# Six RMS norms of a two-block transformer kernel: squares added on VectorE before TensorE sums their partitions

## The chip, the cores and the metric

The kernel runs on one core of a Trainium2 chip. The core has a matrix engine (TensorE, PE in the profile), a vector engine (VectorE, DVE), a scalar engine (ScalarE, ACT), GpSimd (POOL) and SyncE (SP), which here issues most of the DMAs. Each engine takes its instructions in a fixed order and stops where one has to wait for another engine. Matrix products go to PSUM, everything else lies in SBUF. The metric is the device time of one execution in microseconds (us).

## The reference

A first block (convolution and attention, then a product-key mixture of experts called peer) and a second block of two layers, on 256 tokens of 1024 features. Ahead of nearly every sublayer stands the same norm, whose result is scaled and shifted:

```python
def rms_norm(x, g):
    xf = x.astype(jnp.float32)
    y = xf * lax.rsqrt(jnp.mean(xf * xf, axis=-1, keepdims=True) + EPS)
    return (y * g.astype(jnp.float32)).astype(x.dtype)

def modulate_2(h, shift, scale):
    return h * (1 + scale[:, None, :]) + shift[:, None, :]

    for layer in range(DEPTH_2):        # cut from second_block
        if layer == N_A_LAYERS:
            k_sh, v_sh, F_sh = shared_kv(x, c_act, kv_ada_w, kv_ada_b, kv_norm_g, kv_w, fgate_w, fgate_b)
        h = modulate_2(rms_norm(x, norm_g[layer, 0]), sh1, sc1)
        x = x + 0.5 * g1[:, None, :] * swiglu(h, ffn_w_in[layer, 0], ffn_w_out[layer, 0])
        h = modulate_2(rms_norm(x, norm_g[layer, 1]), sh2, sc2)
        ...                             # mix = diff_attention(h, ...) or forgetting_attention(h, ...)
        x = x + g2[:, None, :] * mix
        h = modulate_2(rms_norm(x, norm_g[layer, 2]), sh3, sc3)
        x = x + 0.5 * g3[:, None, :] * swiglu(h, ffn_w_in[layer, 1], ffn_w_out[layer, 1])
```

## The kernel before

The program runs through the stages mix, peer, f00, diff, f01, kv, f10, forget and f11. The fNN are the feed-forward sublayers, diff and forget the two attentions, kv makes the keys, values and forget gate that forget uses. The stream X lies in SBUF as eight tiles of 128 features by 256 tokens (KT = 8, P = 128, T = 256), so the sum over the features of one token runs over the eight tiles and over the partitions of each.

Products are made with split operands: a weight chunk of 128x1024 comes by DMA into `raw`, ScalarE rounds it to `whi`, VectorE makes the rest `wlo = raw - whi`, and TensorE adds hi x hi, lo x hi and hi x lo. A product of one chunk with all of X is 24 matmuls of 128x256 (258 with two columns for the shift) and is called a unit here; its result lies in one PSUM buffer. Two buffers of the pool `ps_mm` and one or two of others hold such results, so a further unit can't start until an earlier one's buffer has been read.

A norm is begun by `norm_begin` (line 480). It makes `xg`, X times the gain, split in hi (ScalarE) and lo (VectorE), with a high scheduling priority (NPRIO = 400). ScalarE then squares X, one tile 128x256 at a time, into `sq`, and TensorE multiplies each with a matrix of ones: the eight `ss` matmuls, in plain fp32, add up the squares over all features and put the sum of each token on every partition. ScalarE takes the root, VectorE the reciprocal, which gives `rstd`, called `r` in the code.

The first units of the stage don't wait for `rstd`. They multiply the weights with `xg`, which is not normalised, and `fixed` (line 530) puts it right afterwards on VectorE: `fixb` copies the column of the shift out of PSUM, `fix` multiplies the product with `rstd`. When both have read it, the PSUM buffer is free. These units are called `wq` in peer, `qkv` in diff, `gux` in the feed-forwards, `kvu` in kv and `bq` in forget. Meanwhile `norm_steps` (line 540) makes the normalised h, tile by tile, over a scratch tile `nt`, for all later units.

`norm_begin` is called by peer (line 1605), the feed-forwards (line 590), diff (747), kv (907) and forget (1025). With `fin`, in f00, it also makes the final norm of the first block, with sixteen `ss`. f10 has no norm of its own; kv's serves it. The order of instructions on each engine is set ahead of time by a scheduler, which takes what it holds to be ready by its own estimates, and by priorities (`high_priority`; FPRI = 100 for `fixed`). On the chip that order is fixed. All operations go through one helper, so nearly every row of the profile has line L263.

Of the kernel before, what the change touches and what calls it, by code (L numbers as in the profile page):

```python
# [9 lines left out]
F32 = mybir.dt.float32  # L10
# [4 lines left out]
AF = mybir.ActivationFunctionType  # L15
# [5 lines left out]
P = 128  # L21
T = 256
D = 1024
KT = 8
# [125 lines left out]
class Ring:  # L150


    def __init__(self, pool, n):
        self.order = [pool] * n
        self.n = n
# [126 lines left out]
class Kern:  # L282
# [3 lines left out]
    def __init__(self, nc, tc, ins, out, phases, ctx):  # L286
        self.nc, self.tc, self.ins, self.out, self.ctx = nc, tc, ins, out, ctx
        self.phases = phases
        e = ctx.enter_context
        self.p_const = e(tc.tile_pool(name="const", bufs=1))  # L290
        self.r_raw = Ring(e(tc.tile_pool(name="raw", bufs=self.NRAW)), self.NRAW)
        self.r_w = Ring(e(tc.tile_pool(name="wsplit", bufs=self.LOOK + 1)), self.LOOK + 1)
        self.p_h = e(tc.tile_pool(name="hsplit", bufs=1))
        self.p_s = e(tc.tile_pool(name="small", bufs=2))
        self.ps_mm = e(tc.tile_pool(name="ps_mm", bufs=2, space=PSUM))
        self.ps_bg = e(tc.tile_pool(name="ps_bg", bufs=2, space=PSUM))
        self.bg = []
        self.gprio = {}
        self.late = []
        self.ada_done = {}  # L300
        self.ada_raw = {}
        self.cb2 = self.ada_last = None
        self.prio = 0
        self.lead = {"s": [], "v": [], "t": []}
        self.pace, self.paces = {}, {}
        self.nc = PacedNC(self, nc)
        self.xg = self.p_n = self.masks = None
        self.h_ready = self.fin_pending = False


# [169 lines left out]
    def norm_begin(self, pool, G, sh, xg, fin=None, psq=None):  # L480


        nc = self.nc
        hi, lo = xg
        x = self.X
        sh2 = pool.tile([P, KT, 2], F32, tag="sh2", name="sh2", bufs=1)
        nc.vector.memset(sh2, 0.0)
        nc.vector.tensor_copy(sh2[:, :, 0], sh)
        nc.scalar.activation(hi[:, :, T:], sh2, AF.Copy)
        nc.vector.tensor_sub(lo[:, :, T:], sh2, hi[:, :, T:])  # L490
        Gx = G
        if fin is not None:
            Gx = self.p_s.tile([P, 8], F32, tag="gcol", name="gcolx")
            nc.vector.tensor_mul(Gx, G, fin)
        n = 1 if fin is None else 2
        ps = self.ps_bg.tile([P, n, T], F32, tag="bg", name="ss")
        nc.scalar.activation(pool.tile([P, 1], F32, tag="sqw", name="sqw", bufs=1), self.eps, AF.Sqrt)
        with self.tc.high_priority(offset=NPRIO):
            for kt in range(KT):
                nc.scalar.activation(hi[:, kt, :T], x[:, kt], AF.Copy, scale=Gx[:, kt:kt + 1])  # L500
                nc.vector.scalar_tensor_tensor(lo[:, kt, :T], x[:, kt], Gx[:, kt:kt + 1], hi[:, kt, :T],
                                               op0=ALU.mult, op1=ALU.subtract)
        fsq = None
        if fin is not None:
            fsq = pool.tile([P, KT], F32, tag="fsq", name="fsq", bufs=1)
            nc.vector.tensor_mul(fsq, fin, fin)
        for kt in range(KT):
            sq = (psq or pool).tile([P, T], F32, tag="sq", name="sq", bufs=8 if psq else 4)
            nc.scalar.activation(sq, x[:, kt], AF.Square)
            for j in range(n):  # L510
                w = fsq[:, kt:kt + 1].to_broadcast([P, P]) if j else self.ones
                nc.tensor.matmul(ps[:, j], w, sq, start=kt == 0 and j == 0, stop=kt == KT - 1, skip_group_check=n > 1)
        r = pool.tile([P, T], F32, tag="rstd", name="rstd", bufs=1)
        r0 = pool.tile([P, T], F32, tag="r0", name="r0", bufs=1)
        with self.tc.high_priority(offset=NPRIO):
            if fin is None:
                nc.scalar.activation(r0, ps[:, 0], AF.Sqrt, scale=1.0 / D, bias=self.eps)
                nc.vector.reciprocal(r, r0)
                return Gx, r

            ms = pool.tile([P, T], F32, tag="ms", name="ms", bufs=1)
            nc.vector.tensor_scalar(ms, ps[:, 0], 1.0 / D, EPS, op0=ALU.mult, op1=ALU.add)
            m2 = pool.tile([P, T], F32, tag="ms2", name="ms2", bufs=1)
            nc.vector.tensor_scalar(m2, ms, EPS, None, op0=ALU.mult)
            nc.vector.scalar_tensor_tensor(m2, ps[:, 1], 1.0 / D, m2, op0=ALU.mult, op1=ALU.add)
            nc.scalar.activation(r0, m2, AF.Sqrt)
            nc.vector.reciprocal(r, r0)
        return Gx, r, ms
# [11 lines left out]
    def norm_steps(self, pool, x, G, sh, hi, lo, r):  # L540
        nc = self.nc
        for kt in range(KT):
            t = pool.tile([P, T], F32, tag="nt", name="nt", bufs=4)
            nc.vector.scalar_tensor_tensor(t, x[:, kt], G[:, kt:kt + 1], r, op0=ALU.mult, op1=ALU.mult)
            nc.scalar.activation(hi[:, kt], t, AF.Identity, bias=sh[:, kt:kt + 1])
            nc.vector.scalar_tensor_tensor(lo[:, kt], t, sh[:, kt:kt + 1], hi[:, kt], op0=ALU.add, op1=ALU.subtract)
            yield
# [1504 lines left out]
```

## Time and profile before

| | us |
|---|---|
| three runs | 2185.59, 2186.04, 2186.75; median 2186.04 |
| the profiled execution: time, and its span | 2187.28, 2185.5 |
| TensorE busy (matmuls) | 2152.6, 98% of the span |
| VectorE busy | 1763.1, 81% |
| ScalarE busy | 1202.3, 55% |
| granted TensorE clock, mean | 0.997 |

All durations come from the profiled execution. Its time is 1.78 us above its span. The chain of waits is the work that ended last, followed back in time step by step. A row of a timeline or of a group gives an instruction as `out<-in` with the shape and type, and behind it, in brackets, the idle time before it and what ended that. An fp32 matmul with plain operands leaves two records, one with split operands leaves one.

### The profile page before, as it was taken

The numbers are of one execution on the slowest core, as the hardware profiler recorded it, in microseconds if no ns is written. First come the engines' busy times: TensorE is split into PE (matmuls) and PEld (weight loads), VectorE is DVE, ScalarE is ACT, GpSimd is POOL, SyncE is SP. The second block draws the span as 40 slices with busy tenths as digits, with TensorE's granted clock in tenths as the row PEclk, the third lists the DMA queues.
The fourth block names the chain that finished last, engine by engine and source line by source line (L and its number), as shares of the span: only waits on it lengthen the run. The fifth ranks groups of instructions, "written<-read, shape, count | busy, mean of one in ns | idle before, by whom it ended". The sixth has DMA issues, their size and how long they took to land.

```text
span 2185.5 us, 39500 instructions
## 1 busy us (share of the span) xinstructions
PE 2152.6 (98%) x16034; PEld 2021.8 (93%) x16034; DVE 1763.1 (81%) x3214; ACT 1202.3 (55%) x1946; POOL 11.4 (1%) x26
## 2 busy tenths in 40 slices
PE   7999999999999999999999999999999999999998
PEld 4887899999999999999999999999999999999997
DVE  7779689987888777657779987879887899798665
ACT  5677665444434444444446556766556555576554
POOL 0000000000000000000000000000000000000000
PEclk9999999999999999999999999999999999999999
DMA  8246354545445988857776985436885688724551
GB/s 322 78 183 231 116 176 155 193 174 185 173 155 197 311 302 304 246 208 270 287 277 241 358 315 207 146 137 229 296 305 181 229 325 330 269 97 174 193 183 49
DMA packets 100631, 481.08 MB, mean 220 GB/s; under 512 B 40832, under 2 KB 41368, under 8 KB 44960
## 3 DMA queue, kind: packets, MB, share of 16 engines
q1 hardware_dynamic: 95744, 462.70, 58.7%
q10 hardware_dynamic: 3456, 10.90, 1.3%
q0 software_dynamic: 1248, 4.95, 0.6%
q8 instruction: 126, 2.06, 0.4%
q14 instruction: 57, 0.47, 0.1%
HBM read 469.05 MB, written 11.04 MB: 220 GB/s over the span
## 4 chain that ended last, share of the span: by engine, by line
PE 89%; DVE 7%; ACT 2%; issue 1%; DMA 1%; DVEq 0%; ACTq 0%
PE acc L263 28%; PE gu L263 20%; PE u L263 15%; PE win L263 4%; PE gps L263 3%; PE qkv L263 2%; PE gux L263 2%; DVE wlo L263 2%; PE pacc L263 2%; PE kvu L263 2%; PE ss L263 2%; PE sc L263 1%; PE po L263 1%; ACT whi L263 1%; DVE A L263 1%; PE outs L263 1%
## 5 line engine op out<-in xcount | busy, mean ns | idle before, releaser
L263 DVE TENSOR_TENSOR wlo<-raw,whi 128x1024 fp32r<-128x1024 f32 x650 | 794.1, 1224 | 233.6 <-ACT whi L263 228.7
L263 ACT ACTIVATE whi<-raw 128x1024 fp32r<-128x1024 f32 x650 | 686.5, 1057 | 483.9 <-PE acc L263 139.1
L263 PE MATMUL gu<-h,whi 128*128 128x512 f32 x1264 | 443.4, 393 | 0.0
L263 PE MATMUL u<-h,whi 128*128 128x256 f32 x2048 | 379.6, 284 | 1.6 <-ACT whi L263 1.6
L263 PE MATMUL gu<-h,wlo 128*128 128x256 f32 x1264 | 354.0, 280 | 0.0
L263 PEld LDWEIGHTS u<-h,whi 128*128 128x128 f32 x2048 | 322.9, 192 | 1.8 <-ACT whi L263 1.8
L263 PE MATMUL acc<-wh,whi 128*128 128x256 f32 x1024 | 289.8, 283 | 0.4 <-ACT wh L263 0.4
L263 PE MATMUL acc<-wh,wlo 128*128 128x256 f32 x1024 | 289.7, 283 | 0.0
L263 PE MATMUL acc<-wl,whi 128*128 128x256 f32 x1024 | 289.5, 283 | 0.0
L263 PEld LDWEIGHTS gu<-h,whi 128*128 128x128 f32 x1264 | 236.7, 187 | 50.2
L263 DVE SCALAR_TENSOR_TENSOR junk<-raw,crow 128x1024 f32<-128x1024 f32 x198 | 241.8, 1221 | 19.9 <-DMA raw<-wts 11.1
L263 PE MATMUL u<-h,wlo 128*128 128x256 f32 x1024 | 252.1, 284 | 0.2 <-DVE wlo L263 0.2
L263 PEld LDWEIGHTS gu<-h,wlo 128*128 128x128 f32 x1264 | 238.7, 189 | 0.0
L263 PE MATMUL acc<-ah,whi 128*128 128x256 f32 x704 | 197.6, 281 | 0.0
L263 PEld LDWEIGHTS acc<-wh,whi 128*128 128x128 f32 x1024 | 196.6, 192 | 0.6 <-ACT wh L263 0.6
L263 PEld LDWEIGHTS u<-h,wlo 128*128 128x128 f32 x1024 | 195.8, 191 | 1.2 <-DVE wlo L263 0.9
L263 PE MATMUL acc<-ah,wlo 128*128 128x256 f32 x704 | 196.9, 280 | 0.0
L263 PEld LDWEIGHTS acc<-wh,wlo 128*128 128x128 f32 x1024 | 196.6, 192 | 0.0
L263 PEld LDWEIGHTS acc<-wl,whi 128*128 128x128 f32 x1024 | 196.5, 192 | 0.0
L263 PE MATMUL acc<-al,whi 128*128 128x256 f32 x704 | 195.9, 279 | 0.4
L263 PEld LDWEIGHTS acc<-ah,whi 128*128 128x128 f32 x704 | 132.2, 188 | 3.4
L263 PEld LDWEIGHTS acc<-al,whi 128*128 128x128 f32 x704 | 132.1, 188 | 1.0 <-DVE al L263 1.0
(386 smaller groups left out, 3590.9 us busy)
## 6 DMA issues: line engine op xcount, KB each, us to landing
raw<-wts SPq DMA_DIRECT2D x427, 1024.0 KB, 5.0
G<-sp ACTq DMA_DIRECT2D x16, 512.0 KB, 3.0
gl<-G SPq DMA_DIRECT2D x16, 512.0 KB, 6.9
Fb<-fscr POOLq DMA_DIRECT2D x1, 2048.0 KB, 8.7
scr<-brow POOLq DMA_DIRECT2D x1, 1536.0 KB, 20.4
KR<-wts SPq DMA_DIRECT2D x1, 1024.0 KB, 10.9
KS<-wts SPq DMA_DIRECT2D x1, 1024.0 KB, 12.9
X<-xT SPq DMA_DIRECT2D x1, 1024.0 KB, 14.8
```

The source lines that it names most:

```text
L263: i = f(*a, **kw)
```

## The change

In the six norms without `fin` (peer, diff, f01, kv, forget, f11), ScalarE squares four tiles of X with one instruction into `sqn`, one tile of 128 x 8 x 256. VectorE adds them in place: tiles 2 and 3 to 0 and 1, 6 and 7 to 4 and 5, then 4 and 5 to 0 and 1, each with one instruction of 128x512. TensorE then sums the partitions of tiles 0 and 1 alone, with two `ss`. In f00 the eight squares and sixteen `ss` stay, with slices of `sqn` as their target. `norm_steps` uses the first four slices of `sqn` as its scratch once that tile exists.

```diff
--- before.py
+++ after.py
@@ -304,7 +304,7 @@
         self.lead = {"s": [], "v": [], "t": []}
         self.pace, self.paces = {}, {}
         self.nc = PacedNC(self, nc)
-        self.xg = self.p_n = self.masks = None
+        self.xg = self.p_n = self.masks = self.sqn = None
         self.h_ready = self.fin_pending = False
 
 
@@ -504,12 +504,24 @@
         if fin is not None:
             fsq = pool.tile([P, KT], F32, tag="fsq", name="fsq", bufs=1)
             nc.vector.tensor_mul(fsq, fin, fin)
-        for kt in range(KT):
-            sq = (psq or pool).tile([P, T], F32, tag="sq", name="sq", bufs=8 if psq else 4)
-            nc.scalar.activation(sq, x[:, kt], AF.Square)
-            for j in range(n):
-                w = fsq[:, kt:kt + 1].to_broadcast([P, P]) if j else self.ones
-                nc.tensor.matmul(ps[:, j], w, sq, start=kt == 0 and j == 0, stop=kt == KT - 1, skip_group_check=n > 1)
+
+        sqn = self.sqn = pool.tile([P, KT, T], F32, tag="sqn", name="sqn", bufs=1)
+        if fin is None:
+
+            for i in (0, 4):
+                nc.scalar.activation(sqn[:, i:i + 4], x[:, i:i + 4], AF.Square)
+                nc.vector.tensor_add(sqn[:, i:i + 2], sqn[:, i:i + 2], sqn[:, i + 2:i + 4])
+            nc.vector.tensor_add(sqn[:, 0:2], sqn[:, 0:2], sqn[:, 4:6])
+            for i in range(2):
+                nc.tensor.matmul(ps[:, 0], self.ones, sqn[:, i], start=i == 0, stop=i == 1)
+        else:
+            for kt in range(KT):
+                sq = sqn[:, kt]
+                nc.scalar.activation(sq, x[:, kt], AF.Square)
+                for j in range(n):
+                    w = fsq[:, kt:kt + 1].to_broadcast([P, P]) if j else self.ones
+                    nc.tensor.matmul(ps[:, j], w, sq, start=kt == 0 and j == 0, stop=kt == KT - 1,
+                                     skip_group_check=n > 1)
         r = pool.tile([P, T], F32, tag="rstd", name="rstd", bufs=1)
         r0 = pool.tile([P, T], F32, tag="r0", name="r0", bufs=1)
         with self.tc.high_priority(offset=NPRIO):
@@ -540,7 +552,7 @@
     def norm_steps(self, pool, x, G, sh, hi, lo, r):
         nc = self.nc
         for kt in range(KT):
-            t = pool.tile([P, T], F32, tag="nt", name="nt", bufs=4)
+            t = pool.tile([P, T], F32, tag="nt", name="nt", bufs=4) if self.sqn is None else self.sqn[:, kt % 4]
             nc.vector.scalar_tensor_tensor(t, x[:, kt], G[:, kt:kt + 1], r, op0=ALU.mult, op1=ALU.mult)
             nc.scalar.activation(hi[:, kt], t, AF.Identity, bias=sh[:, kt:kt + 1])
             nc.vector.scalar_tensor_tensor(lo[:, kt], t, sh[:, kt:kt + 1], hi[:, kt], op0=ALU.add, op1=ALU.subtract)
```

With other dependencies the scheduler also arrives at another order. First TensorE at the start of diff, before. `ss` are the sums of squares, `qkv_N` the units (`xg0` and `xg1` are the hi and lo part of X times gain, `whi` and `wlo` the weights); left out are the matmuls between.

```order
L263 MATMUL ss_15361<-sq_15380,ones_78 128x256
L263 MATMUL qkv_15427<-xg0_13151,whi_15230 128x258
...
L263 MATMUL ss_15361<-sq_15383,ones_78 128x256
L263 MATMUL qkv_15427<-xg0_13151,whi_15230 128x258
...
L263 MATMUL ss_15361<-sq_15386,ones_78 128x256
...
L263 MATMUL ss_15361<-sq_15401,ones_78 128x256
L263 MATMUL qkv_15427<-xg1_13152,whi_15230 128x258 x8
L263 MATMUL qkv_15464<-xg0_13151,whi_15253 128x258
...
L263 MATMUL qkv_15464<-xg1_13152,whi_15253 128x258 x8
L263 MATMUL qkv_15499<-xg0_13151,whi_15284 128x258
...
L263 MATMUL qkv_15499<-xg1_13152,whi_15284 128x258 x8
L263 MATMUL qkv_15536<-xg0_13151,whi_15288 128x258
```

The same place after:

```order
L263 MATMUL qkv_15387<-xg0_13142,whi_15206 128x258
...
L263 MATMUL qkv_15459<-xg1_13143,whi_15260 128x258 x8
L263 MATMUL qkv_15618<-xg0_13142,whi_15418 128x258
L263 MATMUL ss_15337<-sqn_15356,ones_78 128x256 x2
L263 MATMUL qkv_15618<-xg0_13142,wlo_15419 128x258
...
L263 MATMUL qkv_15618<-xg1_13143,whi_15418 128x258 x8
L263 MATMUL qkv_15496<-xg0_13142,whi_15264 128x258
```

The eight `ss` stood inside the first unit. The two stand behind three whole units and the first matmul of a fourth, `qkv_15618`. That is the unit which used to be further back: it has a PSUM buffer of another pool, and its 24 matmuls are pulled ahead of `qkv_15496`, the unit that needs the buffer of the first one.

VectorE at the same place, from the last splits of weights ahead of the reciprocal to the first two `fix`, before:

```order
L263 TENSOR_TENSOR wlo_15289<-raw_15058,whi_15288 128x1024
L263 TENSOR_TENSOR wlo_15424<-raw_15087,whi_15423 128x1024
L263 COPY fixb_15452<-qkv_15427 128x1
L263 RECIPROCAL rstd_15404<-r0_15405 128x256
L263 TENSOR_TENSOR wlo_15459<-raw_15087,whi_15458 128x1024
L263 TENSOR_TENSOR fix_15453<-qkv_15427,rstd_15404 128x256
L263 COPY fixb_15489<-qkv_15464 128x1
L263 TENSOR_TENSOR fix_15490<-qkv_15464,rstd_15404 128x256
```

And after, from the first `fixb` on:

```order
L263 COPY fixb_15412<-qkv_15387 128x1
L263 COPY fixb_15449<-qkv_15424 128x1
L263 TENSOR_TENSOR sqn_15356<-sqn_15356 128x512 x2
L263 TENSOR_TENSOR wlo_15384<-raw_15063,whi_15383 128x1024
L263 TENSOR_TENSOR sqn_15356<-sqn_15356 128x512
L263 COPY fixb_15484<-qkv_15459 128x1
L263 TENSOR_TENSOR wlo_15419<-raw_15063,whi_15418 128x1024
L263 TENSOR_TENSOR wlo_15456<-raw_15124,whi_15455 128x1024
L263 TENSOR_TENSOR wlo_15491<-raw_15124,whi_15490 128x1024
L263 RECIPROCAL rstd_15364<-r0_15365 128x256
L263 TENSOR_TENSOR wlo_15555<-raw_15178,whi_15554 128x1024
L263 TENSOR_TENSOR fix_15413<-qkv_15387,rstd_15364 128x256
```

One `wlo` stood between `rstd` and the first `fix`, and two ahead of `rstd`. Now the three additions stand among the `wlo`, three `wlo` come between the last addition and `rstd`, and `wlo_15555` stands ahead of `fix_15413`; its operand `whi_15554` is made by ScalarE in the buffer of `whi_15418`, which the unit `qkv_15618` reads. The second `fixb` stands ahead of the additions and reads the result of the second unit. forget and kv have the same pattern in this order.

VectorE at the start of f01, before:

```order
L263 TENSOR_TENSOR wlo_16966<-raw_16502,whi_16965 128x1024
L263 TENSOR_TENSOR wlo_17099<-raw_16610,whi_17098 128x1024
L263 RECIPROCAL rstd_17085<-r0_17086 128x256
L263 COPY fixb_17127<-gux_17102 128x1
L263 TENSOR_TENSOR wlo_17133<-raw_16610,whi_17132 128x1024
L263 TENSOR_TENSOR fix_17128<-gux_17102,rstd_17085 128x256
```

and after:

```order
L263 TENSOR_TENSOR wlo_16918<-raw_16454,whi_16917 128x1024
L263 COPY fixb_17063<-gux_17038 128x1
L263 TENSOR_TENSOR sqn_17013<-sqn_17013 128x512 x2
L263 COPY fixb_17105<-gux_17074 128x1
L263 TENSOR_TENSOR wlo_17035<-raw_16562,whi_17034 128x1024
L263 TENSOR_TENSOR sqn_17013<-sqn_17013 128x512
L263 TENSOR_TENSOR wlo_17069<-raw_16562,whi_17068 128x1024
L263 TENSOR_TENSOR wlo_17117<-raw_16708,whi_17116 128x1024
L263 RECIPROCAL rstd_17021<-r0_17022 128x256
L263 COPY fixb_17151<-gux_17120 128x1
L263 TENSOR_TENSOR fix_17064<-gux_17038,rstd_17021 128x256
```

Here `fixb_17105`, the copy from the second unit, and one `wlo` stand between the second and the third addition, and on TensorE the two `ss` follow right behind the second unit. f11 has the same order.

## Rows read from the trace of the kernel before

**Rows 1.** The page: busy time of the engines; shares of the chain by engine.
```profile
PE 2152.6 (98%) x16034; PEld 2021.8 (93%) x16034; DVE 1763.1 (81%) x3214; ACT 1202.3 (55%) x1946; POOL 11.4 (1%) x26
...
PE 89%; DVE 7%; ACT 2%; issue 1%; DMA 1%; DVEq 0%; ACTq 0%
```

**Rows 2.** Stretches: us; busy (instructions) of PE, PEld, DVE, ACT, POOL; clock, DMA share, GB/s.
```profile
20.00:38.90 18.90, 12.34 (x44) 4.85 (x42) 16.47 (x36) 8.70 (x14) 0.00 (x0) 1.00 0.79 281
38.90:45.80 6.90, 6.04 (x24) 5.45 (x25) 6.90 (x18) 2.56 (x5) 0.33 (x1) 0.51 0.92 381
345.00:365.00 20.00, 17.99 (x146) 17.36 (x146) 20.00 (x105) 8.73 (x15) 0.00 (x0) 1.00 0.36 125
352.00:358.00 6.00, 4.14 (x33) 3.94 (x34) 6.00 (x33) 2.85 (x5) 0.00 (x0) 1.00 0.29 90
1340.00:1400.00 60.00, 59.66 (x450) 56.72 (x450) 53.89 (x129) 44.98 (x106) 0.00 (x0) 1.00 0.40 141
1400.00:1480.00 80.00, 78.66 (x614) 74.91 (x615) 59.10 (x141) 56.34 (x141) 0.00 (x0) 1.00 0.37 133
1660.00:1700.00 40.00, 39.36 (x311) 37.62 (x311) 30.90 (x65) 28.66 (x50) 1.09 (x2) 1.00 0.43 153
1950.00:1985.00 35.00, 35.00 (x284) 32.22 (x284) 30.07 (x82) 21.92 (x56) 0.00 (x0) 1.00 0.34 122
```

**Rows 3.** The chain: start us, us, what; from peer, diff, f01, kv and forget.
```profile
307.05 1.01 DVE A L263 x4
...
1353.21 0.43 PE ss L263 x2
...
1356.26 2.59 PE ss L263 x12
1358.85 7.09 PE qkv L263 x59
1365.94 0.45 PE sc L263 x4
...
1477.60 1.29 PE ss L263 x6
...
1679.18 2.83 PE fgp L263 x24
...
1915.06 5.76 PE bq L263 x48
1920.82 1.31 PE sc L263 x8
```

**Rows 4.** Tiles: count, then ns min/median/max, first and last start in us.
```profile
L263 PE MATMUL ss<-sq,ones x144: 377/379/483, 19.6 to 2175.8; 128*128 128x256 f32 x144
...
L263 ACT ACTIVATE sq<-X x62: 401/404/422, 18.5 to 2173.1; 128x256 f32<-128x256 f32 x62
...
L263 DVE TENSOR_TENSOR A<-A,gl x32: 684/686/689, 712.5 to 920.4; 128x512 f32<-128x512 f32 x32
...
L263 DVE RECIPROCAL rstd<-r x9: 1744/1753/1755, 28.2 to 2176.7; 128x256 f32<-128x256 f32 x9
L263 DVE TENSOR_TENSOR fix<-qkv,rstd x9: 412/417/419, 1363.1 to 1389.1; 128x256 f32<-128x256 f32 x9
```

**Rows 5.** The page's costliest groups: busy us, mean ns, idle before and releaser.
```profile
L263 DVE TENSOR_TENSOR wlo<-raw,whi 128x1024 fp32r<-128x1024 f32 x650 | 794.1, 1224 | 233.6 <-ACT whi L263 228.7
L263 ACT ACTIVATE whi<-raw 128x1024 fp32r<-128x1024 f32 x650 | 686.5, 1057 | 483.9 <-PE acc L263 139.1
```

**Rows 6.** Timeline of VectorE where diff starts: start us, us, instruction [idle before].
```profile
1357.44 2.35 DVE L263 TENSOR_TENSOR wlo<-raw,whi 128x1024 fp32r<-128x1024 f32 x2
...
1360.35 1.75 DVE L263 RECIPROCAL rstd<-r 128x256 f32<-128x256 f32 x1 [0.34 <-ACT r L263]
```

**Rows 7.** Timeline of VectorE where peer starts.
```profile
302.56 1.75 DVE L263 RECIPROCAL A<-A 128x256 f32<-128x256 f32 x1 [1.80 <-ACT A L263]
...
304.75 0.41 DVE L263 TENSOR_TENSOR A<-wq,A 128x256 f32<-128x256 f32 x1
```

## The prediction

> **What bounds the kernel now.** First the page's busy times and the chain of waits: TensorE is busy for 2152.6 of 2185.5 us and carries 89% of the chain that ended last [rows 1]. A 98% average could hide stages with other limits, so next comes the table of stretches. Around five of the six norms TensorE is nearly full: 59.66 of 60 us where diff starts, 39.36 of 40 where kv starts, 35.00 of 35 at the end of forget [rows 2]. The exception is the routing in peer: between 345 and 365 us VectorE is busy for all 20 us and TensorE for 17.99 [rows 2], and the chain goes over VectorE there [rows 3]. So in five stages an instruction taken off TensorE gives its time back, provided that no new wait takes it, and in peer only what VectorE's line allows. The chain also shows that TensorE does not wait for the norm today: from the last `ss` at 1358.85 us it runs 59 `qkv` matmuls without a break [rows 3]. The products run on unnormalised X; 1/rms is multiplied in afterwards by `fix`, which frees a PSUM buffer. The room for that is what the change works with.
>
> **What is removed.** Six norms lose 6 of 8 `ss` matmuls, 36 in all. The trace has two records for each fp32 matmul (the 72 of the program with `sq` and `ones` are x144 [rows 4]), and 12 records take 2.59 us on the chain [rows 3]: 0.216 a record, 0.432 us a matmul. Per norm 6 x 0.432 = 2.59 us, in all 36 x 0.432 = 15.55 us of TensorE. ScalarE's 8 squares of 0.404 us become two of 128x1024; the row of that size is `whi` with 1.057 us [rows 4, 5], so 3.23 becomes 2.11 us a norm. ScalarE idles by turns around the norms, and that saving I count as nothing.
>
> **What is added.** Three VectorE additions 128x512 a norm. A row of that form and type exists, `A<-A,gl` with 0.686 us [rows 4]; queued ones start about 0.6 us apart by the overlap of the rows of [rows 6], where two `wlo` of 1.22 take 2.35. Some 2 us a norm, 12.3 us in all by the full duration. VectorE is off the chain in the five stages, so they cost what they delay.
>
> **What moves, and this decides.** The scheduler puts the pair of `ss` where it thinks the sums ready: behind 73 unit matmuls in diff, kv and forget, behind 48 in f01 and f11, behind 34 in peer; before it was inside the first unit. On VectorE the sums stand between splits of weights (`wlo`) and `COPY fixb`, which waits for the end of a unit on TensorE; RECIPROCAL then stands behind three more `wlo` (two in f01). The first `fix` comes later than the third PSUM buffer is full, and TensorE must stop, for the first time. One unit is 24 matmuls; 48 took 5.76 us in forget [rows 3], so 2.88 a unit.
>
> *diff.* TensorE starts its units at 1353.2 us, where the first `ss` stands now [rows 3]. With about 0.3 us for the late half of `xg` (a wide square stands between), unit 1 ends at 1359.3 and unit 2 at 1362.1. VectorE ends `xg` at 1357.4 [rows 6], does a `wlo` and waits for unit 1: COPY 1359.4, two additions 1360.7, `wlo` (1.15 queued) 1361.85, third addition 1362.5. `ss` waits 0.35 us and ends at 1363.4. Then COPY and the `wlo` of the unit pulled forward: 1363.8, again 0.35 us of wait. Two `wlo` more, 1366.1; RECIPROCAL 1.75 us [rows 4, 6], 1367.85. That unit ends at 1366.55 (1363.8 + 23 x 0.12); only then may its buffer take the next split: `whi` 1.06 to 1367.65, `wlo` to 1369.0, `fix` 0.42 [rows 4] to 1369.4. TensorE waits 1369.4 - 1366.55 = 2.85 us for its next PSUM buffer. New idle 3.55, saved 2.59: +0.95 us.
>
> *forget* has the same order of instructions and, by the same steps 0.35 + 0.35 + 2.9 = 3.6: +1.0.
>
> *f01.* Two units from 1477.6 [rows 3] end at 1483.4. The pair of `ss` comes next and needs COPY 0.15, `wlo` 1.2, addition 0.7 and the hand-overs: 2.15 us idle to 1485.5; `ss` to 1486.4, unit 2 to 1489.3. RECIPROCAL stands behind two `wlo`, 1487.8 to 1489.55, COPY and `fix` to 1490.1: 0.8 us idle. In all 2.95: +0.4. *f11* alike: 3.05, +0.45.
>
> *kv.* The same order on VectorE, but TensorE has the forget gate's 24 matmuls (2.83 us [rows 3]) and the pulled unit to run meanwhile: only the wait of `ss`, 0.37. Net -2.2.
>
> *peer.* TensorE would idle 3.6 us, but the line that counts is VectorE's. Before it idles by turns up to 306 us and then is full [rows 2, 7]. After, the first `fix` comes at 308.2 instead of 304.75, yet two `wlo` of later units and the additions have used that time: what was done at 310.1 us is done at about 310.2 to 310.5. I take +0.4, nearer to VectorE's line; at worst it is the whole 3.6 - 2.59 = +1.0, at best nothing, if the additions fall wholly into idle time: a gain is excluded, since TensorE waits for VectorE's results later in the stage anyway (2.01 of the 20 us [rows 2]).
>
> Sum: 0.4 + 0.95 + 0.4 - 2.2 + 1.0 + 0.45 = +1.0 us. f00 keeps its 16 `ss`; its operands only change place, zero. Of the profiled 2187.28 us this makes 2188.3; that execution lies 1.24 above the median 2186.04, so the median should go to 2187.0. The six waits add up to 3.6 + 3.55 + 2.95 + 0.37 + 3.6 + 3.05 = 17.1 us. Their bounds: none, which leaves the whole -15.55; and each half as long again, +8.6 on top of +1.0.
>
> **A rule weighed.** Between 20 and 38.9 us TensorE was busy for 12.34 of 18.9 us, and then the granted clock was 0.51 for 6.9 us, the lower of the two levels, 1.2 GHz; between 352 and 358 it was busy for 4.14 of 6 us, and the clock stayed at 1.00 [rows 2]. The Trainium skill (TensorE: Matmul & The Clock Gate, "HAM oscillation — how this bites in real kernels") describes a kernel in which each wait for data sends TensorE back to half its clock, and it pays again in every round. By that rule each of the long new waits would cost more than itself; by the row of 352 to 358 it does not. The third rival is this case.
>
> **Rivals.**
> 1. *The waits are mostly hidden.* If the first `fix` comes in time in diff, f01, forget and f11 as it does in kv, each of the five leaves 2.2 us: 5 x -2.2 + 0.4 = -10.6, 2175.4; with peer also, at the limit, 2170.5. For it: kv has just this, and ScalarE and VectorE have idle time around [rows 6, 7]. Against: in the new order `fix` stands behind three to four `wlo` of 1.15 us, whatever the pace of the rest.
> 2. *Late heads and pairs (the other side).* The first score matmul comes at 1365.94 in diff and 1920.82 in forget [rows 3]; with `fix` at 1369.4 they start some 4.5 us later. If the softmax chains don't catch up, the last heads are that late when the output product needs them: 2 x 4.5 = +9, 2196.0. It decides where VectorE has under 4.5 us of slack behind. For it: VectorE is busy for 53.89 of 60 us in 1340 to 1400 [rows 2]. Against: 59.10 of 80 us in 1400 to 1480 and 30.07 of 35 in 1950 to 1985 [rows 2], and the `wlo` that stand ahead of `fix` are work that later need not be done.
> 3. *The clock falls.* 6.9 us at 0.51 lose about 3.4 us [rows 2]. In diff, f01, forget and f11, and once more in peer: 5 x 3.4 = 17, 2204. Against: the clock row of 352 to 358.
> 4. *It does less than it says*: the chip takes as long for two `ss` at their new place as for eight, say because they wait for weights. Then the 15.55 us are not there: +1.0 + 15.55 = +16.6, 2202.6. Little speaks for it: `ss` matmuls follow each other by a steady 0.216 a record [rows 3].
>
> **How the numbers follow.** A measurement of this kernel can tell about 0.2% (4.4 us) from no change. Forecast, small loss and gain that cancel: 0.50, of which 0.42 is within 4.4 us and 0.04 to either side. Rival 1: 0.20 (0.17 faster, 0.03 same, since partly hidden waits give less). Rival 2: 0.21 (0.16 slower, 0.05 same). Rival 3: 0.05, rival 4: 0.04, both slower. That makes faster 0.21, same 0.50, slower 0.29. The range reaches from partly hidden waits (-7, 2179) to the late heads (+9, 2196); beyond it lie the limit of rival 1 and rivals 3 and 4, some 0.18. The forecast's own range is 2182 to 2191.
>
> **What would show it.** TensorE's busy time some 15 us lower and its idle time as much higher, with rows in which `qkv`, `bq` and `gux` wait for `fix` 2 to 3 us once a stage and `ss` waits for `sqn`, longest in f01 and f11. RECIPROCAL of `rstd` in diff near 1366 instead of 1360.35. In kv no wait beyond 0.4. Wrong: no idle time before the units' matmuls (rival 1), waits of `sc`, `ot` or `po` in the second half of diff and forget (rival 2), a granted clock under 1.00 after 320 us (rival 3).

## The result

| | us |
|---|---|
| before | 2185.82 median (2185.49 to 2186.75, 4 runs) |
| changed | 2198.93 median (2197.67 to 2201.34, 4 runs) |
| ratio | 1.0059, 95% interval 1.0046 to 1.0072 |
| the profiled execution of the changed kernel: time, span | 2198.02, 2195.8 |

The change made the kernel 13.1 us slower. The forecast was 2187.0 with a range of 2179 to 2196. In the profiled executions the span grew by 10.3 us. The page of the changed kernel, to hold against [rows 1]:

```profile
PE 2148.4 (98%) x15962; PEld 2016.5 (92%) x15962; DVE 1773.5 (81%) x3232; ACT 1196.0 (54%) x1910; POOL 11.5 (1%) x26
...
PE 88%; DVE 8%; ACT 2%; issue 1%; DMA 1%; DVEq 0%; ACTq 0%
```

TensorE lost 72 records, as the change says, 36 matmuls with an expected 15.55 us. Its busy time fell by only 4.2, and its idle time (span less busy) rose from 32.9 to 47.4 us. The new idle time was foreseen; that the busy time hardly fell was not. Here is what TensorE waited for in the changed kernel, with total, count and longest wait in us. In peer `fix` writes into the tile `A`. None of the first five stands in the list of before, and the wait of `lft` (for the forget gate, in kv) was 0.5 us there:

```profile
PE ss L263 <- DVE sqn L263: 4.9, 5, 2.3
...
PE wq L263 <- DVE A L263: 3.4, 1, 3.4
...
PE bq L263 <- DVE fix L263: 2.8, 1, 2.8
PE qkv L263 <- DVE fix L263: 2.8, 1, 2.8
...
PE gux L263 <- DVE fix L263: 1.3, 2, 0.7
PE lft L263 <- DVE lf L263: 1.3, 1, 1.3
```

Forecast and measured wait can be set side by side: `ss` 0.35, 0.35, 0.37 and twice about 2.2, in all some 5.5 against 4.9; `wq` 3.6 against 3.4; `qkv` and `bq` 2.85 and 2.9 against 2.8 each; `gux` 0.8 in f01 and about as much in f11 against two of together 1.3. The steps behind them are to be seen on VectorE where diff starts (the answer to [rows 6]):

```profile
1359.79 0.16 DVE L263 COPY fixb<-qkv 128x1 f32<-128x1 f32 x1 [0.39 <-PE qkv L263]
1359.87 1.28 DVE L263 TENSOR_TENSOR sqn<-sqn 128x512 f32<-128x512 f32 x2
1361.07 1.22 DVE L263 TENSOR_TENSOR wlo<-raw,whi 128x1024 fp32r<-128x1024 f32 x1
1362.20 0.68 DVE L263 TENSOR_TENSOR sqn<-sqn 128x512 f32<-128x512 f32 x1
...
1362.88 3.48 DVE L263 TENSOR_TENSOR wlo<-raw,whi 128x1024 fp32r<-128x1024 f32 x3
1366.28 1.74 DVE L263 RECIPROCAL rstd<-r 128x256 f32<-128x256 f32 x1
1368.30 1.22 DVE L263 TENSOR_TENSOR wlo<-raw,whi 128x1024 fp32r<-128x1024 f32 x1 [0.28 <-ACT whi L263]
1369.44 0.75 DVE L263 TENSOR_TENSOR fix<-qkv,rstd 128x256 f32<-128x256 f32 x2
```

The reader is to see `fixb` waiting for TensorE, the additions behind it, three `wlo` in one row of 3.48 us, RECIPROCAL at 1366.28 (1360.35 before; 1366.1 in the forecast), and a `wlo` ahead of `fix`. TensorE's row for it:

```profile
1370.00 0.55 PE L263 MATMUL qkv<-xg,whi 128*128 128x258 f32 x1 [2.83 <-DVE fix L263]
```

So the waits came as worked out. The forecast did not have what followed them. These stretches are the waits and what lay behind them (columns as in [rows 2]; the granted clock is the third number from the end):

```profile
307.80:311.20 3.40, 3.40 (x18) 3.40 (x17) 3.40 (x13) 2.60 (x7) 0.00 (x0) 0.50 0.00 0
1367.20:1370.00 2.80, 0.00 (x0) 0.03 (x1) 2.52 (x4) 1.17 (x2) 0.00 (x0) 0.88 1.01 413
1370.00:1376.10 6.10, 6.10 (x28) 6.10 (x29) 4.12 (x12) 2.82 (x7) 0.00 (x0) 0.50 0.13 54
1486.90:1489.30 2.40, 0.35 (x3) 0.14 (x2) 2.16 (x5) 1.30 (x2) 0.00 (x0) 1.00 0.73 300
1489.30:1496.00 6.70, 5.99 (x45) 5.74 (x46) 6.47 (x11) 3.04 (x4) 0.00 (x0) 1.00 0.53 197
1693.60:1697.00 3.40, 3.40 (x18) 3.40 (x18) 1.76 (x7) 2.17 (x3) 0.00 (x0) 0.50 0.00 0
1926.80:1929.50 2.70, 0.00 (x0) 0.00 (x0) 2.44 (x4) 1.07 (x2) 0.00 (x0) 0.92 1.00 419
1929.60:1932.50 2.90, 2.90 (x12) 2.71 (x13) 0.55 (x2) 2.08 (x5) 0.00 (x0) 0.50 0.22 90
```

With the waits in peer, diff and forget the clock fell to 0.50, that is 1.2 of 2.4 GHz, for 3.4, 6.8 and 3.4 us by the trace: in peer 0.6 us behind the wait, in diff and forget in its last 0.7 and 0.5 us. Once the waits were over TensorE was busy throughout. In kv it fell too, at 1693.6, 1.5 us behind the wait of 1.3 us for `lft`. In f01 a wait of 2.1 us left it at 1.00 in this execution. In the kernel before it was 1.00 through all of this. The low clock lasted 17.1 us; 1.2 of them lay inside waits. At the low clock the unit matmuls start 0.214 us apart (16 in the 3.4 us of kv; the row's x18 counts two that were still running), against 0.12 at the full one (48 in 5.76 us [rows 3]), so that about (17.1 - 1.2) x (1 - 0.12 / 0.214) = 7.0 us were lost by it. They sit in the busy time and are the larger part of the 11.4 us by which that failed to fall.

Now by stage. A stage ends with the last update of X that it makes. These rows have the first and last of such updates in the changed kernel:

```profile
L263 DVE SCALAR_TENSOR_TENSOR X<-acc,half,X x32: 474/476/485, 1351.8 to 2183.8; 128x256 f32<-128x256 f32 x32
...
L263 DVE SCALAR_TENSOR_TENSOR X<-pacc,mods,X x16: 473/477/487, 1477.9 to 1993.8; 128x256 f32<-128x256 f32 x16
...
L263 DVE SCALAR_TENSOR_TENSOR X<-pj,mods,X x8: 475/478/486, 278.1 to 296.8; 128x256 f32<-128x256 f32 x8
```

The last `pj` is 1.2 us earlier than before (298.0), in the stage mix, which the change doesn't touch and whose length varies by some us between the profiles (-1.4 to +3.0 against before); the last `pacc` is 9.3 later (1984.5) and the last `acc` 10.4 (2173.4). The same for every stage, each stage's length less that of before, in us, for the changed kernel, and for kernels of the experiments (the profiled execution of each):

| stage | forecast | changed | changed, run again | fillall | late | best |
|---|---|---|---|---|---|---|
| peer | +0.4 | +2.0 | +1.9 | +0.2 | -0.8 | -0.6 |
| f00 | 0 | -0.1 | -0.1 | -0.1 | -0.1 | -0.1 |
| diff | +0.95 | +3.1 | +1.7 | +0.8 | -0.8 | -1.3 |
| f01 | +0.4 | +0.4 | +1.9 | +0.4 | -0.1 | -2.6 |
| kv and f10 | -2.2 | -0.1 | -0.2 | -1.6 | -2.3 | -2.2 |
| forget | +1.0 | +5.4 | +5.4 | +3.9 | +3.3 | -0.5 |
| f11 | +0.45 | +1.0 | +1.0 | +1.0 | +2.4 | -1.6 |
| sum | +1.0 | +11.6 | +11.6 | +4.5 | +1.7 | -8.9 |
| of this at clock 0.5 | 0 | 17.1 | 17.1 | 0 | 3.4 | 0 |

The last row is not a loss but a length: the us between 300 and 2170 at the low clock.

### The profile page after: what moved, and what is told of

The parts are those of the page before. It is cut to its first block, busy times and chain, and to the rows that moved or that the text cites. A ratio compares the mean times of both kernels' runs of the same rounds, so it can differ in the third digit from the quotient of the medians.

```text
span 2195.8 us, 39369 instructions
## 1 busy us (share of the span) xinstructions
PE 2148.4 (98%) x15962; PEld 2016.5 (92%) x15962; DVE 1773.5 (81%) x3232; ACT 1196.0 (54%) x1910; POOL 11.5 (1%) x26
## 4 chain that ended last, share of the span: by engine, by line
PE 88%; DVE 8%; ACT 2%; issue 1%; DMA 1%; DVEq 0%; ACTq 0%
PE acc L263 28%; PE gu L263 20%; PE u L263 15%; PE win L263 4%; PE qkv L263 3%; DVE wlo L263 3%; PE gps L263 2%; PE gux L263 2%; PE kvu L263 2%; PE pacc L263 2%; PE sc L263 2%; DVE A L263 1%; PE po L263 1%; PE outs L263 1%; PE bq L263 1%; ACT whi L263 1%
```

## The experiments

Theory A: the change costs through waits that its late `rstd` makes, and most of it through the clock that falls behind them. Theory B: the late order itself costs, the heads and pairs that start later above all, and the clock is a side effect. Theory C: three additions on VectorE for six `ss` are a bad trade in any order.

**Useless work in two waits (fill), then in five (fillall).** Behind the unit at whose end TensorE waits, matmuls without any use are placed (shown as they stand in fillall, and their call in forget):

```diff
+    def filler(self, ps, n):
+        last = self.lead["t"][-1]
+        with self.tc.high_priority(offset=NPRIO):
+            for i in range(n):
+                m = self.nc.nc.tensor.matmul(ps, self.ones, self.X[:, 0, :P], start=True, stop=True)
+                if i == 0:
+                    self.tc.add_manual_dep(m.ins, last.ins.name, NOSYNC, reason="order")
...
+                fl = t == 5
+                ps = pool.tile([P, T + 2 + P * fl], F32, tag=tag, name="bq")
+                self.mm_unit(ps[:, :T + 2], w, self.xg)
+                if fl:
+                    self.filler(ps[:, T + 2:], 12)
```

> The changed kernel, and behind the unit that was pulled forward in diff and in forget TensorE gets twelve useless matmuls 128x128 (about 12 x 0.22 = 2.6 us) that lie in the 2.83 us in which it waited for fix. Nothing else is altered; peer and kv stay as they are. Theory A (the wait sends the granted clock to 0.5, and that is most of the loss): the clock stays at 1.00 in diff and forget, where it was 0.5 for 6.83 and 3.41 us, the waits are gone from the list or under 0.4 us, and the time falls by 3.4 + 1.7 = 5.1 us, to about 2194, although work was added; peer and kv keep their 3.41 us at 0.5. Theory B (the late rstd delays heads and pairs, and the clock is a side effect): no gain, 2199, or some tenths more.

Measured: 2196.23 (2194.19 to 2198.50), ratio to before 1.0047, 1.0033 to 1.0061. In the profile the waits for `fix` in diff and forget are gone and the clock stays at 1.00 there; the stages come to +0.8 and +4.0 instead of +3.1 and +5.4. In kv, which has no filler, the clock did not fall in this execution either, against what was expected. The whole time is 2.7 us lower instead of 5, and the interval overlaps that of the changed kernel: waits remained in peer, f01, kv and f11. So the same in five places, with the changed kernel run again beside it:

> The changed kernel unaltered, as the measure for the other kernels of this batch on the same chip. Both theories: about 2199, with the clock at 0.5 for 3.4 or 6.8 us behind some of the waits of 2.8 and 3.4 us.

Measured: 2198.35 (2197.80 to 2201.30), ratio 1.0058, 1.0044 to 1.0071.

> The changed kernel with useless 128x128 matmuls in five of its new waits: 14 in peer, 12 in diff and forget, 9 in f01 and f11 (about 12.8 us of work that gives nothing), each behind the unit at whose end TensorE waited. Theory A (the clock that falls behind the waits is the larger part of the loss): no 0.5 between 300 us and the end except perhaps in kv, and the time falls by 5 to 7 us against the same kernel without them, to 2192 to 2194. Theory B (the waits and the late order themselves are the loss): no gain, or slower by the few tenths by which a filler outlasts its wait.

Measured: 2192.68 (2191.71 to 2195.05), ratio 1.0028, 1.0016 to 1.0041. Matmuls of 13.3 us by the trace were added, and the kernel became 5.7 us faster than without them; the slowest run is faster than the fastest without. The filler in diff, the waits of the kernel, and the stretches around the five places:

```profile
1366.60 2.84 PE L546 MATMUL qkv<-X,ones 128*128 128x128 f32 x24
```

```profile
PE gux L263 <- DVE fix L263: 1.3, 2, 0.7
PE lft L263 <- DVE lf L263: 1.3, 1, 1.3
...
PE ss L263 <- DVE sqn L263: 0.8, 4, 0.2
...
PE wq L263 <- DVE A L263: 0.3, 1, 0.3
```

```profile
304.80:312.00 7.20, 6.92 (x60) 6.75 (x60) 6.81 (x19) 3.55 (x7) 0.00 (x0) 1.00 0.41 148
1364.80:1378.00 13.20, 13.04 (x107) 12.62 (x106) 12.45 (x30) 8.33 (x17) 0.00 (x0) 1.00 0.40 156
1487.00:1496.00 9.00, 8.33 (x67) 8.07 (x66) 8.84 (x17) 5.69 (x10) 0.00 (x0) 1.00 0.44 147
1920.00:1935.00 15.00, 14.85 (x119) 14.33 (x118) 12.07 (x30) 11.29 (x26) 0.00 (x0) 1.00 0.37 141
1995.00:2008.00 13.00, 11.93 (x92) 11.25 (x92) 12.47 (x26) 8.31 (x14) 0.00 (x0) 1.00 0.64 222
```

The clock reads 1.00 in each. With the clock out of it, the stages stand at the forecast within 0.6 us in all but forget (table), and their sum is 7.1 us below that of the changed kernel, as the 7.0 worked out above. Of these, 1.5 us are kv's, which has no filler: its wait of 1.3 us for `lft` is still there, and the clock did not fall behind it this time. Theory A holds; what is left in forget is not the clock. The changed kernel's second profile shows that the fall is not the same each time: f01's wait of 2.1 us kept the clock in the first, and in this one

```profile
1486.90:1489.20 2.30, 0.92 (x5) 0.87 (x5) 2.30 (x4) 0.38 (x1) 0.00 (x0) 0.99 0.80 335
1489.30:1492.60 3.30, 3.30 (x17) 3.30 (x16) 2.77 (x2) 0.47 (x1) 0.00 (x0) 0.50 0.63 211
```

it did not, while diff had 3.4 us at 0.5 instead of 6.8.

**The two heads of a pair (popair, fillpair).** What is left in forget? `po` are the value products of a pair of heads, `pacc` the output product that follows. The chain of before has the `po` of a pair in 0.81 us for 8 records (start, us, what), here that of the last pair:

```profile
1977.17 0.81 PE po L263 x8
```

and that of the changed kernel at the end of forget:

```profile
1978.61 0.81 PE po L263 x4
1979.43 0.31 PE pacc L263
1979.74 0.79 PE po L263 x4
...
1986.70 1.57 PE po L263 x8
```

The two heads write different halves of the partitions, 64 and 64. Before, their matmuls stand together in all eight pairs. In the new order one other matmul stands between them in two pairs, and then each head takes the 0.8 us that both took. A scheduling edge puts them together again:

```diff
-                        nc.vector.tensor_copy(WT[:, m], pt)
+                        both = nc.vector.tensor_copy(WT[:, m], pt)
...
+                    if m == 0:
+                        self.tc.add_manual_dep(mm.ins, both.ins.name, NOSYNC, reason="order")
```

> The changed kernel with one scheduling edge: in forget the value matmuls po of a pair's first head may not be scheduled before the operand of the second head is there, so that the four matmuls of a pair stand together in TensorE's order (in the changed kernel another matmul stands between the heads in two of eight pairs). Theory A2 (matmuls of two heads that write different halves of the partitions run side by side only if nothing stands between them): the po of each pair take 0.8 us for 8 records, as in the kernel before, in place of 1.6 us in the split pairs, and forget is 1.6 us shorter: 2197.3. Rival (the clock alone explains forget): the po rows stay as they are and the time is the same, 2199.

Measured: 2198.30 (2195.53 to 2199.24), ratio 1.0052, 1.0038 to 1.0065: too little to tell by the time. In the profile the two pairs take 1.01 and 0.92 us, and forget is 1.7 us shorter, +3.7.

> The kernel with useless matmuls in five waits, and the po matmuls of a pair together. If what is left in forget there (3.9 us against before) is for 1.6 us the two split pairs: forget 2.3 us, the time 2191. If it is the late start of the pairs alone: 2192.7 as without.

Measured: 2191.31 (2190.54 to 2193.09), ratio 1.0022, 1.0013 to 1.0031; forget at +2.35, 1.6 us below fillall, as expected. The time alone does not show it, since the two intervals overlap; in this execution the clock fell in kv (-0.2 instead of -1.6), and the sum of the stages is the same as in fillall, +4.5. Of the last 1.4 us above the forecast in forget, 0.3 (0.2 before) and 0.5 are waits at its end, of `po` for its operand and of `pacc` for the last h, and 0.76 the last pair, 1.57 us although its matmuls stand together. Why it ran one head after the other is not settled. Of theory B no more than these 1.4 us are left.

**The order (prio, priopair, late).** prio puts squares, additions and `ss` under the priority of `xg`; priopair adds popair's edge.

```diff
         if fin is None:
-            for i in (0, 4):
+            with self.tc.high_priority(offset=NPRIO):
+                for i in (0, 4):
...
```

> The changed kernel with squares, additions and the two ss under the same scheduling priority as the xg ahead of them (400). In the new order the ss stand behind 42 unit matmuls in diff, kv and forget instead of 73, and one wlo instead of three stands between the last addition and RECIPROCAL. Theory A (what costs is the late place of rstd: waits of 2 to 3 us and the clock that falls behind them): no wait for fix above 1 us and no 0.5 after 320 us, except perhaps in peer; the 15.55 us saved come through less about 4 us of short waits and up to 4 us of po pairs that stand apart in this order: 2174 to 2182. Theory C (three additions on VectorE and fewer ss are a bad trade in any order): 2186 or more.

Measured: 2189.91 (2186.98 to 2193.18), ratio 1.0015, 1.0006 to 1.0024. A miss: 9 us better than the change, but 8 to 16 above what was expected. f01 gave back 2.5 us, all of it. In diff and forget TensorE waited 1.8 us for a `wlo` behind `fixb`, in f11 1.8 us for `fix`, in peer 3.4 us as before; the clock fell in peer and forget.

> prio and the edge of popair together. Theory A2: 1 to 4 us below prio, since five of eight po pairs stand apart there: 2171 to 2180. Rival: the same as prio.

Measured: 2188.30 (2185.98 to 2191.66), ratio 1.0004, 0.9995 to 1.0013; forget +0.8 instead of +5.7, and all eight pairs stand together. The difference to prio is in the range of theory A2 (the intervals overlap), but the time lies 8 us above what was expected: the waits of prio remained, and the clock fell in peer, diff, forget and f11.

late leaves the priorities alone and forbids only that `fixb` stands ahead of the RECIPROCAL (which `self.rins` holds; the lines that set it are left out):

```diff
-            nc.vector.tensor_copy(b, ps[:, T:T + 1])
+            c = nc.vector.tensor_copy(b, ps[:, T:T + 1])
+            self.tc.add_manual_dep(c.ins, self.rins.ins.name, NOSYNC, reason="order")
```

> The changed kernel with one scheduling edge: fixb, the copy from a unit's PSUM buffer, may not be scheduled ahead of the RECIPROCAL of its norm, so that VectorE no longer stops for the end of a unit ahead of the additions. Theory A (a copy that waits for TensorE holds up the additions and rstd behind it): ss does not wait in diff and forget and 1.4 us instead of 2.1 to 2.3 in f01 and f11; the first fix comes 1.3 us earlier in diff and forget; 4 us less waiting and fewer falls of the clock, 2190 to 2195. Rival (the additions are late because of xg and wlo, not because of the copy): the waits stay, 2199.

Measured: 2189.08 (2188.00 to 2193.14), ratio 1.0011, 1.0002 to 1.0020. It is more than expected: 9.3 us from an edge on a copy of 0.15 us. In diff the wait for `fix` is 1.5 instead of 2.8 us, `ss` no longer waits there, the wait in peer is 1.6 instead of 3.4, and the clock fell once instead of four times. The `ss` of f01 and f11 still wait 3.7 us together, more than the 2.8 expected. It is not the copy alone: the whole order is another. In diff, counted from the stage's start, the third addition comes 0.6 us earlier than in the changed kernel and RECIPROCAL 0.7, but the first `fix` 2.0, because no `wlo` stands ahead of it any more. In forget three pairs of `po` instead of two stand apart, 0.8 us each.

**ScalarE's part alone (wide8).** Two wide squares, no additions, eight `ss`.

> Only the part on ScalarE: two squares of 128x1024 a norm into the wide tile, no additions, all eight ss. TensorE has the work of the kernel before. Theory A (additions and the ss far behind are what makes rstd late): no new wait over 0.5 us, 2186 to 2188. Rival (the wide square, which has to wait for four tiles, makes rstd late already): waits for fix and 2190 or more.

Measured: 2189.14 (2186.86 to 2193.15), ratio 1.0012, 1.0002 to 1.0021, 1 us above what was expected. In its profile every stage from peer on is within 0.5 us of before and their sum is -0.25; mix, which the edit leaves alone, is 3.0 us longer there, 2.8 of it in a wait of TensorE for the transfer of `hf` (4.1 us instead of 1.3). So the wide squares don't make `rstd` late, and what the timed runs show is not put down to them.

**Versions that could be faster (nopeerlate, best).**

> The new form in diff, f01, kv, forget and f11 and not in peer (which squares eight slices and sums them with eight ss as before); squares, additions and ss at the priority of xg; fixb behind RECIPROCAL; the po matmuls of a pair together. Theory A: with rstd in time the five norms give back most of 5 x 2.59 = 12.9 us, less waits of 0.3 to 1 us each: 2175 to 2181, faster than both kernels. Theory C (additions on VectorE are a bad trade at any place): 2186 or more.

Measured: 2181.22 (2178.72 to 2183.86), ratio 0.9974, 0.9964 to 0.9984.

> The new form in all six norms, fixb behind RECIPROCAL and the po matmuls of a pair together everywhere; squares, additions and ss at the priority of xg in diff, f01, forget and f11, at the plain one in peer and kv, since these two stages came out shortest so (-0.8 and -2.3 us against before in the kernel with fixb behind RECIPROCAL alone). Theory A (waits decide, stage by stage): the sum of the best stages, -0.8 - 1.2 - 2.3 - 2.1 - 0.5 - 1.7 = -8.6, 2176 to 2181, at least as good as the one without peer (2181.2). Rival (the stages hang together, so that a gain in one is lost in the next): 2182 or more.

Measured: 2179.50 (2178.54 to 2181.68), ratio 0.9968, 0.9956 to 0.9981. It keeps the whole change, with `fixb` behind RECIPROCAL, the `po` of a pair together, and the priority in diff, f01, forget and f11:

```diff
         if fin is None:
+            if self.nname in ('peer', 'kv'):
                 for i in (0, 4):
...
+            else:
+                with self.tc.high_priority(offset=NPRIO):
+                    for i in (0, 4):
...
```

VectorE where diff starts in it:

```profile
1355.47 0.68 DVE L263 TENSOR_TENSOR sqn<-sqn 128x512 f32<-128x512 f32 x1
...
1357.29 0.69 DVE L263 TENSOR_TENSOR sqn<-sqn 128x512 f32<-128x512 f32 x1
...
1358.30 0.69 DVE L263 TENSOR_TENSOR sqn<-sqn 128x512 f32<-128x512 f32 x1
1358.90 1.67 DVE L263 SCALAR_TENSOR_TENSOR xg<-X,gcol,xg 128x256 fp32r<-128x256 f32 x4
1360.49 2.35 DVE L263 TENSOR_TENSOR wlo<-raw,whi 128x1024 fp32r<-128x1024 f32 x2
1362.76 1.75 DVE L263 RECIPROCAL rstd<-r 128x256 f32<-128x256 f32 x1
1364.42 0.16 DVE L263 COPY fixb<-qkv 128x1 f32<-128x1 f32 x2
1364.54 0.76 DVE L263 TENSOR_TENSOR fix<-qkv,rstd 128x256 f32<-128x256 f32 x2
```

The additions lie among the `xg`, RECIPROCAL follows two `wlo`, and `fix` starts 1.8 us behind the start of RECIPROCAL. Page and waits of TensorE:

```profile
PE 2138.1 (98%) x15962; PEld 2007.6 (92%) x15962; DVE 1770.3 (81%) x3232; ACT 1196.7 (55%) x1910; POOL 11.4 (1%) x26
```

```profile
PE hf_ps L263 <- DMA hf<-hf: 5.3, 1, 5.3
...
PE wq L263 <- DVE A L263: 1.6, 1, 1.6
...
PE lft L263 <- DVE lf L263: 1.1, 1, 1.1
PE bq L263 <- DVE fix L263: 1.0, 1, 1.0
PE qkv L263 <- DVE fix L263: 1.0, 1, 1.0
```

Busy is 14.5 us below before (2152.6): the 15.55 us come through where the clock stays. Of the waits that the change makes, 1.6 us in peer, 1.0 each in diff and forget and 1.1 for `lft` (0.5 before) are left; the 5.3 us for `hf` lie in mix. Theory C is out: the same additions and the same `ss` make the kernel 6.8 us faster than before. The kernel before with the same edges and priorities was not run; that they alone would make it faster is not excluded, but its list has no wait for `fix` or `sqn` that they could remove.

## Why the prediction was wrong

- *The terms of the change were right.* 36 matmuls less; waits of 17.1 us forecast and 15.2 measured; RECIPROCAL and `fix` in diff within 0.5 us. (The prediction counts units from 0 where it writes "unit 1" and "unit 2".) With the clock held up by filler the stages came to +0.2, +0.8, +0.4, -1.6 and +1.0 against +0.4, +0.95, +0.4, -2.2 and +0.45 forecast (peer, diff, f01, kv, f11).
- *The step that failed* stands under "A rule weighed" and in rival 3: "by the row of 352 to 358 it does not", with a chance of 0.05. A wait was priced at its own length, and the low clock behind it at nothing. The clock fell in four places of the first profile and cost about 7.0 us; filling the waits with useless work, which shortens no path, gave 5.7 us back in the timed runs. The row of 352 to 358 could not carry the step: its 1.86 idle us lay in two gaps, the longer 1.5 us, while five of the new waits are 2.1 to 3.4 us in one piece. Taken over all kept traces between 300 and 2165 us, the clock fell in or within 1.8 us behind each of the 12 single waits of 2.8 and 3.4 us, behind 7 of 15 of 1.8 to 2.3 us, and behind none of 23 of 1.5 and 1.6 us. Length alone does not decide it, though: behind the wait for `lft` in kv it fell in 5 of 9 that lasted 1.3 to 1.4 us. The estimate of the rival itself, 5 x 3.4 = 17 us, was too high: there were four falls, three of 3.4 us and one of 6.8, and a fall of 3.4 us costs about 1.5.
- *The Trainium skill* (TensorE: Matmul & The Clock Gate, "HAM oscillation — how this bites in real kernels") describes a kernel that pays anew with half the clock after each wait for data. The trace agrees behind the waits of 2.8 and 3.4 us in both profiles of the changed kernel, and only at times behind those of 2.1 to 2.3.
- *forget was mis-sized*, +1.0 for what is +3.9 without the clock. 1.6 us were `po` pairs that the new order took apart, a term that the prediction didn't have: it looked at the order where diff, f01 and forget start, and not at the rest of forget. 0.8 us of waits at the end of forget are rival 2, late pairs, at a fraction of the 4.5 us it was priced at, and 0.76 are the last pair, whose cause is open; diff caught up wholly.
- *kv* gave -1.6 to -2.3 in fillall, late and best, where the clock stayed, near the -2.2 forecast, and -0.1 where it fell behind a wait for the forget gate that had grown from 0.5 to 1.3 us; the forecast had no wait beyond 0.4 there.
- Rival 1 (waits hidden) and rival 4 (it does less than it says) did not come. That the waits can be avoided, and the saving then appears, was shown by best.

## What to carry to other kernels

On an engine that is 98% busy, work taken away is worth its time only if nothing has to wait for the result longer than it did: follow the freed instruction's consumer through the queue of every engine it passes, and look for a copy or a split that waits in between. Price a new wait of TensorE, where it is longer than any that the kernel had there, at its length and the low clock that may follow, and try whether useless matmuls in it make the kernel faster; if they do, the wait is the thing to remove. When a scheduler moves a whole stage, compare the order to the stage's end, and look for matmuls that ran side by side only because they stood together.

## What the runs showed of the hardware

- The granted clock fell to 0.50 for 3.4 or 6.8 us with single waits of 2.1 to 3.4 us in a kernel that is otherwise fully busy, behind those of 2.1 to 2.3 not each time, and not at the same place in two executions of the same program; in priopair and prio also in stages with waits of 1.8 us, and in kv behind a wait of 1.3 us.
- 128x128 fp32 matmuls as filler took 2.84 us for 24 records in diff of fillall, 0.12 us a record, and the clock stayed at 1.00.
- At the granted clock of 0.50 the unit matmuls of kv started 0.214 us apart, against 0.12 at 1.00: a low stretch costs about 44% of its length.
- Four fp32 matmuls of two heads that write partitions 0 to 63 and 64 to 127 took 0.81 us together and 0.80 + 0.79 us with one other matmul between the heads.
- A scheduling edge on a copy of 0.15 us moved the kernel by 9.3 us (2198.35 to 2189.08).
